# A static order of instructions, planned with a margin for other engines' answers and a longer load of the inverses' matrices

## The chip, the cores and the metric

The kernel runs on one core of a Trainium2 chip. Times are microseconds (us) on the device for one launch. Where one number stands for a kernel, it is the median of several runs. Engines: PE (TensorE, matmuls), DVE (VectorE), ACT (ScalarE), POOL (GpSimd) and SP (SyncE, which here issues the transfers). Each engine works off its own list of instructions in order.

## What is computed

One layer over 2048 tokens of width 1024, all in float32:

```
h = rms_norm(x);  proj = h @ w_in            # 17 chunks of 128 columns
A: sliding-window attention, 6 query heads, window 128, in blocks of 128 queries
B: RWKV-7 time mixing, 6 heads of 64: S = S*d + (S a) b^T + v k^T;  y = S r,  then GroupNorm, bonus, gate
M: cross-attention of 4 heads into 256 memory tokens
x = x + concat(A, B, M) @ w_out
u = rms_norm(x) @ w_up;  uc = conv3(u);  x = x + (silu(gate) * val) @ w_down     # 2816 columns wide
```

## The kernel before

Large products run in a split form: each float32 operand is cut into a high part (whi, hh, h2h, made by ACT) and a low part (wlo, hl, h2l, made by DVE as the rest), and three matmuls stand for one. The feed-forward products go by Strassen's scheme: seven products of half blocks (tiles uf, uch, uip in PSUM) for eight; DVE forms sums of weight pieces (ws) for them, and three buffers hold split weights.

The work has these stages. Up to about 1130 us the projections (tile mm), the attention (pl, lg, tpa, po) and the recurrence run together; the recurrence is cut into 16 blocks of 128 tokens, numbered 0 to 15 here. Then the output projection ends, its result is normalised, the feed-forward's up products run for the two halves of the tokens (44 units, each of which makes two chunks of columns) and last its down products.

In each block of the recurrence twelve small triangular matrices are inverted (rwkv_front_g). PE makes their products (pg), DVE masks them (gmk), two transfers lay them out in DRAM (nbd), and one transfer of 384 KB loads them as nb, with 96 partitions. The tile nb has one buffer, so a load can begin only when the inversion of the block before has read its last row. DVE then makes 31 steps, each one multiplication (xtmp, which reads nb) and one addition (xinv). The inverse goes out to DRAM (xbd), comes back (xa), and is used by the chain of the recurrence (pq, pu, pS, y).

The order of the instructions is static. The code does not call the engines; it records every operation with its engine, an estimated duration, and the operations that it depends on (class Recorder; cost gives the durations, and for a transfer the time that it needs on the way, lat). Then order gives each operation a level, the length of the longest path from it to the end, and run plans the engines in time: on each engine that is free it takes, of the operations that are ready by the plan, the one of the highest level. The program is emitted in that order; on the chip the real waits are made by semaphores. So the planner's numbers decide nothing but which instruction stands ahead of which. All instructions are issued from one line, the helper's call in emit (L345 in the profile), so tiles tell them apart, not lines.

Of a transfer the plan takes 900 + SLACK = 2400 ns after it has landed until what waits for it can start, and between engines the fixed answers of the table LAT, 110 to 287 ns.

Of the kernel before, what the change touches and what calls it, by code (L numbers as in the profile page):

```python
# [129 lines left out]
class Recorder:  # L130
# [40 lines left out]
    def add(self, eng, fn, a, k):  # L171
        outs = [v for v in (k.get("out"), k.get("accum_out")) if v is not None] or [a[0]]
        ins = [v for v in list(a) + list(k.values()) if isinstance(v, View) and not any(v is w for w in outs)]
        outs = [v for v in outs if isinstance(v, View)]
        dur, lat = cost(eng, fn, a, k)
        o = self._op(eng, fn, a, k, dur, lat)
        for v, w in [(v, False) for v in ins] + [(v, True) for v in outs]:
            t = v.t
            o.deps.add(t.pool.op)
            if not t.users:  # L180
                t.pool.rings.setdefault(t.tag or t.name, []).append(t)
            box = v.box if t.pool.space != PSUM else tuple((0, n) for n in t.shape)
            keep = []
            for p, b, pw in t.log:
                if (w or pw) and p is not o and all(x0 < y1 and y0 < x1 for (x0, x1), (y0, y1) in zip(b, box)):
                    o.deps.add(p)
                    if w and all(y0 <= x0 and x1 <= y1 for (x0, x1), (y0, y1) in zip(b, box)):
                        continue
                keep.append((p, b, pw))
            keep.append((o, box, w))  # L190
            t.log = keep
            if not t.users or t.users[-1] is not o:
                t.users.append(o)
                t.pool.users.append(o)
        return o
# [12 lines left out]
    def slots(self):  # L208

        for p in self.pools:  # L210
            for tag, ring in p.rings.items():
                held = []
                for t in ring:
# [7 lines left out]
                                u.deps.update(q.users)  # L221
                    held.append(t)

    def delay(self, o, s):
        if o.order or s.order:
            return 0
        return o.lat + 2000 + SLACK if o.lat else self.LAT[o.eng][s.eng]

    def order(self):

# [26 lines left out]
    def run(self):  # L257
        ops = self.ops
        left = {o: len(o.deps) for o in ops}
        now = {e: [] for e in self.ENG}  # L260
        soon = {e: [] for e in self.ENG}
        free = {e: 0.0 for e in self.ENG}
        hw = dma = 0.0
        out = []

        def release(o):

            o.ready = 0.0
            for d in o.deps:
                if d.order:  # L270
                    t = d.start
                elif o.order:
                    t = d.start
                else:
                    t = d.end + (900 + SLACK if d.lat else self.LAT[d.eng][o.eng])
                o.ready = max(o.ready, t)
            if o.eng is None:
                o.start = o.end = o.ready
                out.append(o)
                follow(o)  # L280
            else:
                heapq.heappush(soon[o.eng], (o.ready, o.n, o))

        def follow(o):
            for s in o.succ:
                left[s] -= 1
                if left[s] == 0:
                    release(s)

        for o in ops:  # L290
            if not o.deps:
                release(o)
        while True:
            best = None
            for e in self.ENG:
                if now[e]:
                    t = free[e]
                elif soon[e]:
                    t = max(free[e], soon[e][0][0])
                else:  # L300
                    continue
                if best is None or t < best[0]:
                    best = (t, e)
            if best is None:
                break
            t, e = best
            while soon[e] and soon[e][0][0] <= t:
                o = heapq.heappop(soon[e])[2]
                heapq.heappush(now[e], (-o.level, o.n, o))
            o = heapq.heappop(now[e])[2]  # L310
            if soon[e] and o.dur > 150:
                c = min((c for c in soon[e] if c[0] < t + min(WAIT, o.dur) and c[2].level > o.level), default=None)
                if c:
                    heapq.heappush(now[e], (-o.level, o.n, o))
                    free[e] = c[0]
                    continue
            o.start = t
            if o.lat:
                free[e] = t + (max(o.dur, DMAQ * o.lat) if e == "sync" else o.dur)
                hw = max(hw, t) + 475  # L320
                dma = max(dma, hw + 650) + o.lat
                o.end = dma + (500 if e == "gpsimd" else 0)
            else:
                o.end = free[e] = t + o.dur
            out.append(o)
            follow(o)
        assert len(out) == len(ops)
        return out
# [26 lines left out]


WAIT = 100
SLACK = 1500
WR = 4
WS = 3  # L360
# [13 lines left out]
def cost(eng, fn, a, k):  # L374

    out = k["out"] if "out" in k else a[0]
    n = math.prod(out.shape[1:])
    vecs = sum(isinstance(k.get(v), View) for v in ("scalar", "scalar1", "scalar2", "bias", "scale", "accum_out"))
    src = [v for v in (k.get("in_"), k.get("in0"), k.get("in1")) if isinstance(v, View)]
    psum = any(v.t.pool.space == PSUM for v in src + [out] if isinstance(v, View))  # L380
    if fn == "dma_start":
        v = out if isinstance(out, View) else k["in_"]
        size = max(4 * math.prod(v.shape), 20000)
        return (1050, size / 360) if eng == "gpsimd" else (60, size / 360)
    if eng == "tensor":
        if fn == "transpose":
            return 109, 0
        m, c = math.prod(a[1].shape[1:]), math.prod(a[2].shape[1:])
        if out.box[0][0] >= 64:
            return COL64, 0  # L390
        if a[1].dt == F32R:
            return max(c / 2.4, m / 1.2) + 14, 0
        return 2 * (max(c / 1.2, m / 1.2) + 2), 0
    if fn in ("reduce_max", "reduce_sum"):
        n = math.prod(k["in_"].shape[1:])
    if eng == "gpsimd":
        if k.get("op") == ALU.pow:
            return 300 + 165 * n, 0
        return (150 + 2.1 * n if fn == "tensor_tensor" else 122 + 0.6 * n), 0
    if eng == "scalar":  # L400
        return (50 if psum else 93) + 93 * vecs + n / 1.2, 0
    if fn in ("tensor_scalar", "tensor_copy") and not psum:
        n /= 2
    return 62 + 67 * vecs + n / 0.96 + (7 if fn == "tensor_tensor" else 0), 0
# [1296 lines left out]
```

## Time and profile before

| | us |
|---|---|
| runs | 2533.53, 2536.06 (median), 2548.08 |
| the profiled execution, its own time | 2532.01 |
| its span, first to last instruction | 2530.1 |
| PE busy | 2403.9 (95%) |
| DVE busy | 2037.7 (81%) |
| ACT busy | 1256.3 (50%) |
| mean granted clock of PE | 0.966 |

Busy time of an engine is the time in which it executes an instruction; matmuls overlap, so PE's busy time includes their pipelined ends. The granted clock is given as a share of 2.4 GHz; in any one moment it is either 1.00 or 0.50 (1.2 GHz), so a mean between them tells how long the engine ran at half speed. Stretches of the trace are counted in us from the start of the span.

### The profile page before, as it was taken

The page shows a single profiled execution, that of the slowest core. Times are in us where ns is not written, and L with a number is a line of the kernel's source. Part 1 is how long each engine was busy: PE and PEld are TensorE (multiplying, and loading weights), DVE is VectorE, ACT ScalarE, POOL GpSimd, SP SyncE. Part 2 cuts the span into 40 slices and gives each one's busy share as a digit, 9 for nine tenths or more (in the row PEclk, how much of TensorE's full clock was granted, in tenths as well). Part 3 has the DMA queues.
Part 4 walks back from the last instruction along what each step waited for, and adds up shares of the span by engine and source line. Part 5 has one row for each costly group of instructions (what it writes and reads, how often), then busy time and mean ns, then how long its engine had stood idle before and what let it go on. Part 6 is the DMA issues. An engine that isn't in the chain of part 4 may idle for free.

```text
span 2530.1 us, 36859 instructions
## 1 busy us (share of the span) xinstructions
PE 2403.9 (95%) x12268; PEld 1897.1 (75%) x12268; DVE 2037.7 (81%) x4901; ACT 1256.3 (50%) x2541; POOL 78.5 (3%) x53
## 2 busy tenths in 40 slices
PE   8898999899898989999899999999999998999999
PEld 6777777666676757667788788888888886887887
DVE  6677778778778777769688998899888888878876
ACT  5354544555445554555354455565545463444442
POOL 1111011010000010000000000000000000000000
PEclk9999999989989989999999999999999998999999
DMA  7675745744344464547323733353233256548543
GB/s 230 192 214 153 212 131 149 203 138 121 114 134 124 128 183 137 177 134 259 109 97 111 265 130 106 111 179 137 99 108 106 88 166 205 166 150 274 157 146 111
DMA packets 292935, 389.32 MB, mean 154 GB/s; under 512 B 49911, under 2 KB 155392, under 8 KB 292744
## 3 DMA queue, kind: packets, MB, share of 16 engines
q1 hardware_dynamic: 292744, 386.96, 49.1%
q8 instruction: 97, 1.59, 0.3%
q14 instruction: 94, 0.77, 0.1%
HBM read 274.89 MB, written 111.97 MB: 153 GB/s over the span
## 4 chain that ended last, share of the span: by engine, by line
PE 77%; DVE 9%; DMA 6%; issue 4%; ACT 3%; SPq 0%; POOL 0%; POOLq 0%; DVEq 0%; ACTq 0%
PE uf L345 27%; PE mm L345 15%; PE uch L345 13%; PE uip L345 6%; PE pq L345 4%; DMA nb<-nbd 3%; PE pg L345 2%; PE po L345 2%; DMA wraw<-w_ip_in 2%; DVE wlo L345 1%; DVE uc L345 1%; PE pl L345 1%; PE tpa L345 1%; DVE h2l L345 1%; PE pu L345 1%
## 5 line engine op out<-in xcount | busy, mean ns | idle before, releaser
L345 ACT CAST whi<-wraw 128x512 fp32r<-128x512 f32 (+1 forms) x410 | 250.3, 613 | 367.8 <-PE mm L345 135.2
L345 PE MATMUL uf<-h2h,wlo 128*128 128x512 f32 x1056 | 412.4, 392 | 14.1 <-DVE wlo L345 14.1
L345 PE MATMUL uf<-h2h,whi 128*128 128x512 f32 x1056 | 413.9, 392 | 8.5 <-ACT whi L345 6.0
L345 PE MATMUL uf<-h2l,whi 128*128 128x512 f32 x1056 | 413.0, 391 | 0.0
L345 DVE TENSOR_TENSOR wlo<-wraw,whi 128x512 fp32r<-128x512 f32 (+1 forms) x410 | 277.3, 679 | 101.5 <-ACT whi L345 99.6
L345 ACT CAST whi<-ws 128x512 fp32r<-128x512 f32 (+1 forms) x272 | 164.8, 609 | 348.8 <-PE uf L345 163.7
L345 DVE SCALAR_TENSOR_TENSOR uc<-ub,pp,uc 128x1024 f32<-128x1024 f32 x176 | 225.0, 1282 | 26.2 <-ACT uc L345 25.2
L345 PE MATMUL mm<-hh,whi 128*128 128x512 f32 x544 | 226.7, 418 | 18.6 <-ACT whi L345 6.6
L345 PEld LDWEIGHTS uf<-h2h,wlo 128*128 128x128 f32 x1056 | 199.6, 189 | 57.0 <-DVE wlo L345 15.1
L345 PEld LDWEIGHTS uf<-h2h,whi 128*128 128x128 f32 x1056 | 199.4, 189 | 53.9 <-ACT whi L345 8.1
L345 PEld LDWEIGHTS uf<-h2l,whi 128*128 128x128 f32 x1056 | 199.6, 189 | 41.7 <-DVE h2l L345 0.7
L345 PE MATMUL mm<-hh,wlo 128*128 128x512 f32 x544 | 221.9, 409 | 1.4 <-DVE wlo L345 1.4
L345 PE MATMUL mm<-hl,whi 128*128 128x512 f32 x544 | 223.0, 410 | 0.0
L345 PE MATMUL uch<-h2h,whi 128*128 128x512 f32 x528 | 205.7, 390 | 0.1
L345 PE MATMUL uch<-h2h,wlo 128*128 128x512 f32 x528 | 205.8, 390 | 0.0
L345 PE MATMUL uch<-h2l,whi 128*128 128x512 f32 x528 | 205.5, 389 | 0.0
L345 DVE TENSOR_TENSOR wlo<-ws,whi 128x512 fp32r<-128x512 f32 (+1 forms) x272 | 181.3, 672 | 23.3 <-ACT whi L345 22.0
L345 PEld LDWEIGHTS mm<-hh,whi 128*128 128x128 f32 x544 | 105.9, 195 | 47.1 <-ACT whi L345 8.8
L345 ACT CAST h2h<-tr 128x512 fp32r<-128x512 f32 x182 | 110.3, 620 | 58.5 <-DMA tr<-dg 35.4
L345 DVE TENSOR_TENSOR xtmp<-xinv,nb 96x60 f32<-96x60 f32 (+24 forms) x496 | 100.7, 203 | 38.7 <-DMA nb<-nbd 34.5
L345 DVE TENSOR_TENSOR h2l<-tr,h2h 128x512 fp32r<-128x512 f32 x182 | 120.3, 688 | 9.2 <-ACT h2h L345 9.1
L345 ACT ACTIVATE uc<-ub,pp 128x1024 f32<-128x1024 f32 x88 | 109.7, 1247 | 34.0 <-DVE ub L345 32.9
(366 smaller groups left out, 4721.5 us busy)
## 6 DMA issues: line engine op xcount, KB each, us to landing
wraw<-w_up_in SPq DMA_DIRECT2D x176, 256.0 KB
tr<-dg SPq DMA_DIRECT2D x154, 256.0 KB
wraw<-w_ip_in SPq DMA_DIRECT2D x136, 256.0 KB
dg<-uc SPq DMA_DIRECT2D x88, 256.0 KB
dg<-tt SPq DMA_DIRECT2D x66, 256.0 KB
wraw<-w_op_in SPq DMA_DIRECT2D x64, 256.0 KB
wraw<-w_down_in SPq DMA_DIRECT2D x64, 256.0 KB
xk<-xT_in SPq DMA_DIRECT2D x56, 256.0 KB
```

What stands on the lines that cost most here:

```text
L345: getattr(getattr(nc, o.eng), o.fn)(*map(real, o.a), **{k: real(v) for k, v in o.k.items()})
```

## The change

Two numbers of the planner's model change, and the way in which a long transfer takes up the queue. Between operations of different engines a margin of 300 ns is added to the answer, both in the levels and in the plan. The load of nb gets 2500 ns more on its way; of any transfer's time only 2200 ns occupy the transfers that come after it.

```diff
+    def margin(self, d, o):
+
+        return 0 if d.eng == o.eng or None in (d.eng, o.eng) else MARGIN
+
     def delay(self, o, s):
         if o.order or s.order:
             return 0
-        return o.lat + 2000 + SLACK if o.lat else self.LAT[o.eng][s.eng]
+        return o.lat + 2000 + SLACK if o.lat else self.LAT[o.eng][s.eng] + self.margin(o, s)
...
-                    t = d.end + (900 + SLACK if d.lat else self.LAT[d.eng][o.eng])
+                    t = d.end + (900 + SLACK if d.lat else self.LAT[d.eng][o.eng] + self.margin(d, o))
...
-                dma = max(dma, hw + 650) + o.lat
-                o.end = dma + (500 if e == "gpsimd" else 0)
+                dma = max(dma, hw + 650) + min(o.lat, 2200)
+                o.end = dma + max(0, o.lat - 2200) + (500 if e == "gpsimd" else 0)
...
+MARGIN = 300
...
+        if v.t.name == "nb":
+            return 60, size / 360 + 2500
```

The same instructions are issued, in another order on every engine. Two places show it. The first is DVE in the recurrence, where the inversion of block 5 begins. In the rows, xtmp and xinv are the inversion's steps, nb with its number is the loaded matrix; y, rq_t, rq_y, S0, gam and el belong to the norm and the state of the recurrence, rsb to the attention, wlo, qlo and lo3 are low parts. Between the last xtmp of block 4 and the first of block 5 stand 18 instructions before. These are the last twelve rows of that stretch before:

```order
L345 TENSOR_TENSOR rq_t_4818<-rq_t_4818,rq_y_4809 128x6
L345 TENSOR_TENSOR S0_112<-S0_112,gam_3693 64x3x64
L345 TENSOR_TENSOR vt_4943<-tpv_4871,vm_4905 128x512
L345 TENSOR_SCALAR ss_4926<-ss_4926 128x1
L345 SCALAR_TENSOR_TENSOR rq_y_4809<-rq_t_4818,rq_y_4809 128x6
L345 TENSOR_TENSOR S0_112<-S0_112,gam_3693 64x3x64
L345 TENSOR_TENSOR rq_t_4818<-rq_h_4806,rq_y_4809 128x6
L345 TENSOR_TENSOR rq_t_4818<-rq_t_4818,rq_y_4809 128x6
L345 SCALAR_TENSOR_TENSOR rq_y_4809<-rq_t_4818,rq_y_4809 128x6
L345 TENSOR_TENSOR wlo_4967<-wraw_4837,whi_4955 128x512
L345 TENSOR_TENSOR qlo_4972<-mm_4890,qhi_4965 128x512
L345 TENSOR_TENSOR xtmp_4980<-xinv_4197,nb_4913 96x31
```

With the change 35 instructions stand between the two, and these are the last twelve rows:

```order
L349 TENSOR_TENSOR gam_4558<-el_4583,em__5052 128x3
L349 COPY el_5329<-ep_5042 128x3
L349 TENSOR_TENSOR rq_t_5294<-rq_t_5294,rq_y_5289 128x6
L349 TENSOR_SCALAR rsb_1625<-sx_5265 128x4x2
L349 SCALAR_TENSOR_TENSOR rq_y_5289<-rq_t_5294,rq_y_5289 128x6
L349 TENSOR_SCALAR rsb_1625<-sx_5246 128x4x2
L349 TENSOR_TENSOR qlo_5339<-kp_5291,qhi_5319 128x512
L349 SCALAR_TENSOR_TENSOR y_4943<-y_4943,rq_y_5289,lnw_387 128x64
L349 CAST lo3_5331<-qlo_5339 32x512
L349 SCALAR_TENSOR_TENSOR y_4943<-y_4943,rq_y_5289,lnw_387 128x64 x5
L349 TENSOR_TENSOR y_4943<-y_4943,bv_4812 128x384
L349 TENSOR_TENSOR xtmp_5380<-xinv_4380,nb_5296 96x31
```

The first step of the new inversion has moved back: the end of the norm (the six rows on y and the addition of bv) stands ahead of it now.

The second place is DVE in the feed-forward's first half, where the second half's tokens are normalised (rows uc<-uc,pp, tt) beside the running up products. wlo and ws are pieces of weights that PE waits for, uc<-ub the convolution. Before:

```order
L345 SCALAR_TENSOR_TENSOR uc_15187<-ub_14960,pp_118,uc_15187 128x1024
L345 SCALAR_TENSOR_TENSOR uc_15209<-ub_15094,pp_118,uc_15209 128x1024
L345 TENSOR_TENSOR ws_15241<-ws_15193,wraw_14995 128x512
L345 SCALAR_TENSOR_TENSOR uc_15209<-ub_15094,pp_118,uc_15209 128x1024
L345 SCALAR_TENSOR_TENSOR uc_15196<-uc_15196,pp_118,uc_15064 128x1024
L345 TENSOR_TENSOR uc_15187<-uc_15187,uc_15209 128x1024
L345 TENSOR_TENSOR tt_15261<-uc_15196 128x512
L345 TENSOR_TENSOR tt_15265<-uc_15187,tt_15214 128x512
L345 TENSOR_TENSOR uc_15046<-uc_15187,uc_15046 128x512
L345 TENSOR_TENSOR tt_15273<-uc_15187,tt_15265 128x512
L345 TENSOR_TENSOR wlo_15277<-ws_15241,whi_15247 128x512
```

With the change:

```order
L349 SCALAR_TENSOR_TENSOR uc_15194<-ub_14960,pp_118,uc_15194 128x1024
L349 SCALAR_TENSOR_TENSOR uc_15228<-ub_15101,pp_118,uc_15228 128x1024
L349 SCALAR_TENSOR_TENSOR uc_15177<-uc_15177,pp_118,uc_15071 128x1024
L349 SCALAR_TENSOR_TENSOR uc_15228<-ub_15101,pp_118,uc_15228 128x1024
L349 TENSOR_TENSOR tt_15269<-uc_15177 128x512
L349 TENSOR_TENSOR uc_15194<-uc_15194,uc_15228 128x1024
L349 TENSOR_TENSOR wlo_15276<-ws_15203,whi_15224 128x512
L349 TENSOR_TENSOR tt_15280<-uc_15194,tt_15180 128x512
L349 TENSOR_TENSOR uc_15040<-uc_15194,uc_15040 128x512
L349 TENSOR_TENSOR tt_15286<-uc_15194,tt_15280 128x512
L349 TENSOR_TENSOR wlo_15292<-ws_15188,whi_15242 128x512
```

A wlo has moved into the middle of the pile. Before, fifteen instructions stand between this wlo and the one ahead of it; with the change the longest such stretch around the normalising has ten.

## Rows read from the trace of the kernel before

**Rows 1.** Busy time of each engine (us, instructions), PE's clock, transfers, two stages.
```profile
core 0: us, PE busy (x) PEld busy (x) DVE busy (x) ACT busy (x) POOL busy (x), PEclk, DMA share, GB/s
...
160.00:1050.00 890.00, 820.96 (x5114) 608.18 (x5113) 698.26 (x2652) 457.09 (x1213) 55.09 (x25) 0.93 0.53 151
1050.00:1240.00 190.00, 174.01 (x923) 133.11 (x921) 134.39 (x300) 95.81 (x214) 3.78 (x3) 0.93 0.54 176
```

**Rows 2.** Waits of DVE: us in total, times, longest us.
```profile
DVE xtmp L345 <- DMA nb<-nbd: 34.5, 14, 4.1
```

**Rows 3.** Chain that ended last, at block 5: start us, us, what.
```profile
438.44 7.41 DMA nb<-nbd
...
446.78 0.59 ACT sh L345
```

**Rows 4.** DVE in order of time: blocks 3, 5 (two rows), 15; idle before, releaser.
```profile
344.73 0.19 DVE L345 TENSOR_TENSOR xtmp<-xinv,nb 96x31 f32<-96x31 f32 x1 [4.13 <-DMA nb<-nbd]
...
437.56 0.16 DVE L345 TENSOR_TENSOR xtmp<-xinv,nb 96x8 f32<-96x8 f32 x1
...
445.87 0.19 DVE L345 TENSOR_TENSOR xtmp<-xinv,nb 96x31 f32<-96x31 f32 x1 [2.48 <-DMA nb<-nbd]
...
1025.35 0.18 DVE L345 TENSOR_TENSOR xtmp<-xinv,nb 96x31 f32<-96x31 f32 x1 [3.89 <-DMA nb<-nbd]
```

**Rows 5.** PE in order of time, behind the load of block 5.
```profile
447.42 0.80 PE L345 MATMUL mm<-hh,whi 128*128 128x512 f32 x1 [5.81 <-ACT sh L345]
```

**Rows 6.** Busy time and clock, 30 us behind each load, blocks 0 to 15.
```profile
171.00:201.00 30.00, 27.12 (x121) 21.43 (x120) 24.45 (x90) 14.38 (x26) 8.40 (x2) 1.00 0.53 152
227.00:257.00 30.00, 24.83 (x136) 20.04 (x135) 22.54 (x82) 12.53 (x29) 3.27 (x3) 0.83 0.52 147
293.00:323.00 30.00, 28.93 (x217) 21.35 (x216) 23.11 (x74) 16.75 (x42) 0.00 (x0) 0.94 0.59 170
342.00:372.00 30.00, 27.46 (x174) 20.63 (x172) 25.23 (x90) 17.23 (x42) 8.79 (x2) 0.94 0.46 140
398.00:428.00 30.00, 27.50 (x198) 21.98 (x197) 23.83 (x87) 14.37 (x35) 5.38 (x4) 0.94 0.48 150
443.00:473.00 30.00, 25.58 (x123) 20.86 (x124) 21.87 (x74) 14.13 (x30) 0.64 (x1) 0.89 0.69 187
511.00:541.00 30.00, 27.13 (x188) 20.55 (x189) 20.50 (x93) 18.55 (x59) 6.83 (x1) 0.83 0.43 127
561.00:591.00 30.00, 24.85 (x132) 15.79 (x132) 24.76 (x127) 17.39 (x56) 0.00 (x0) 0.89 0.30 89
629.00:659.00 30.00, 29.64 (x229) 21.71 (x228) 24.65 (x102) 16.62 (x51) 0.18 (x1) 1.00 0.39 116
675.00:705.00 30.00, 23.56 (x100) 13.71 (x98) 22.19 (x112) 14.46 (x49) 0.92 (x1) 0.68 0.33 96
750.00:780.00 30.00, 30.00 (x219) 21.65 (x218) 23.44 (x95) 15.38 (x43) 0.00 (x0) 1.00 0.34 105
799.00:829.00 30.00, 24.70 (x129) 15.55 (x128) 23.76 (x115) 14.61 (x48) 0.00 (x0) 0.83 0.38 105
868.00:898.00 30.00, 30.00 (x212) 21.63 (x211) 23.61 (x98) 17.18 (x49) 0.00 (x0) 1.00 0.37 98
916.00:946.00 30.00, 23.94 (x96) 16.57 (x97) 23.92 (x90) 18.77 (x52) 0.00 (x0) 0.74 0.87 250
981.00:1011.00 30.00, 30.00 (x209) 22.50 (x208) 24.11 (x90) 13.18 (x32) 0.00 (x0) 1.00 0.40 131
1020.00:1050.00 30.00, 26.78 (x150) 20.75 (x148) 25.43 (x115) 16.68 (x51) 0.00 (x0) 0.94 0.63 177
```

**Rows 7.** Busy time and clock, three stretches of the feed-forward.
```profile
1396.00:1412.00 16.00, 11.61 (x40) 8.74 (x39) 16.00 (x24) 4.67 (x8) 0.00 (x0) 0.79 0.71 228
1412.00:2084.00 672.00, 671.63 (x2961) 555.03 (x2960) 600.67 (x931) 362.50 (x535) 0.00 (x0) 1.00 0.39 133
2084.00:2106.00 22.00, 10.29 (x34) 7.96 (x33) 21.27 (x33) 9.65 (x15) 0.00 (x0) 0.69 0.59 192
```

## The prediction

> **What bounds the kernel now.** I read the stages first. From 160 to 1050 us, where the projections, the attention and the recurrent blocks run together, TensorE (PE) is busy 820.96 of 890 us, at a mean granted clock of 0.93 [rows 1]. Busy time times clock is work at full speed: 820.96 x 0.93 = 763.5, so 126.5 us are lost there to waits and to the half clock. In the feed-forward stretch from 1412 to 2084 us PE is busy 671.63 of 672 us at clock 1.00 [rows 7]: an order can win nothing there, only lose. So the change has to earn its time before 1240 us, or at the few marred places after it.
>
> Next, who makes the first of these stages wait. VectorE (DVE) waits 34.5 us in 14 places for one kind of transfer, the load of nb [rows 2]. DVE is in-order and busy 698.26 of 890 us [rows 1], so such a wait holds up all that stands behind. Block 5 shows it. Its load starts at 438.44 and lands 7.41 us later [rows 3]. The inversion before it makes its last step at 437.56; DVE then has work up to 443.4, and stands still for 2.48 us until the first step with the new matrix, at 445.87 [rows 4]. The chain of waits goes from there by way of a sum on DVE, which stood behind that step, to a copy on ScalarE (ACT) at 446.78 [rows 3], for whose answer PE has been idle 5.81 us when it goes on at 447.42 [rows 5].
>
> Then what such a wait costs PE. I cut 30 us behind each of the sixteen loads, from about 5 us after its issue [rows 6], and take 30 minus busy time times clock. In order of the blocks the loss is 2.9, 9.4, 2.8, 4.2, 4.2, 7.2, 7.5, 7.9, 0.4, 14.0, 0, 9.5, 0, 12.3, 0 and 4.8 us, together 87 of the 126.5. The four windows behind the blocks 8, 10, 12 and 14, which wait little or not at all, lose 0.4 us in all: PE can run there at full clock with the same mix of work. The other twelve lose 7.2 each. A wait of two to four us thus brings a loss that is larger than the wait, because the clock drops too: in block 9's window it is 0.68.
>
> **The change, part by part.** No instruction is added or removed; only the order on each engine changes, so the terms are waits.
>
> *The load of nb.* There is one buffer for nb, so a load can start only when the previous inversion has read its last row. For the blocks 3, 5, 7, 9, 11, 13 and 15 this is what binds: the cover is the DVE work between the last xtmp of one inversion and the first of the next. Counted in the built orders that is 12, 18, 21, 14, 27, 15 and 20 instructions before, and 21, 35, 32, 28, 34, 23 and 28 with the change: 127 and 201. In block 5 the instructions from 437.56 to 443.4 took 5.8 us [rows 4], or about 0.32 us each, so the seven covers grow by 74 x 0.32 = 23.7 us, 2.2 to 5.4 us each. The seven waits are 20.6 us together (the first and the last, 4.13 and 3.89 us, in [rows 4]). Block by block the growth covers all of it in 5, 7, 9 and 13, and leaves about 1.2, 0.9 and 1.3 us in 3, 11 and 15: 3.4 us remain, 17.2 go.
>
> The other nine blocks wait 13.9 us. In eight of them the binding piece is the way from the last gmk to the first xtmp; it holds 301 instructions before and 316 with the change, about 0.6 us more each. In block 1 the load now stands behind the previous inversion, with ten instructions between. I let 9 of these 13.9 us stand.
>
> In PE time: the five windows of blocks 5, 7, 9, 11 and 13 lose 7.2 + 7.9 + 14.0 + 9.5 + 12.3 = 50.9 us, two thirds of those of 3 and 15 are 6, and 3 us come from the even blocks: 60 us if all loss in those windows hangs on the load. The other bound is that only the wait itself is won and neither the clock nor what follows: 17 us. Some waits in these windows are of the attention's own chain, so neither end is likely; I take the middle, -38 us.
>
> What holds the new place up: if the covering work were itself late, the wait would only move to it. It is work of the norm (y and its reciprocal root), which needs no transfer, so I let it stand at nothing.
>
> On a rule of the Trainium skill, which speaks against this part: "DMA: Bandwidth & Descriptors", section "Anatomy of one DMA", puts a transfer at about 2.0 us plus its bytes at 436 GB/s; for this load of 384 KB that is an estimate of 2.9 us. By it the old cover of 5.8 us was enough, the longer transfer in the planner would be a false figure, and the term would be nothing. The page's fit is for transfers issued by GpSimd; here the issue is SyncE's, and the trace has 7.41 us, so the measurement decides.
>
> *The margin of 300 ns.* It moves every answer between engines. PE's waits under the load's shadow are the 87 us above; outside those windows the two stages up to 1240 us lose 126.5 - 87 = 39.5 and 190 - 174.01 x 0.93 = 28 us [rows 1]. I see no single place in the order that wins or loses these 68 us. I take nothing, with a quarter of them, 17 us, to either side.
>
> *Feed-forward, normalising the second half.* At 1396 to 1412 us DVE is busy all 16.00 us with 24 instructions, 0.67 us each, while PE loses 16 - 11.61 x 0.79 = 6.8 us [rows 7]. A product is twelve matmuls; at 671.63 / 2961 = 0.227 us each (the steady stretch) it takes 2.72 us, and three buffers of split weights make a reserve of 8.2 us. Before, fifteen DVE instructions stand between two wlo, 10 us: more than the reserve. With the change the most is ten, 6.7 us: less. I take -6, with 0 and -6.8 as bounds.
>
> *From up to down.* At 2084 to 2106 us PE loses 22 - 10.29 x 0.69 = 14.9 us [rows 7]. The pile of DVE work ahead of the first wlo of the down products stays, and grows from 24 to 26 instructions, at 21.27 / 33 = 0.64 us each: +1.5.
>
> Sum: -38 - 6 + 1.5 = -42.5. The profiled execution took 2532.0 us (span 2530.1), 4 us under the median of the three runs. 2532 - 42.5 + 4 gives 2494.
>
> **The rivals.** (1) The load is covered, but the loss in those windows belongs to the attention's chain of answers. Then only the waits are won: -17 - 3 + 1.5, so 2517. For it: a wait of two to four us is a small part of the 7.2 us that such a window loses. Against it: the four good windows hold the same chain and lose 0.4 us.
> (2) No change: what the load no longer holds up waits for something else on DVE's queue, or the loads land later still because others were moved ahead of them on SyncE's queue; also the skill's figure, which would make the first term nothing (I give that 0.04 within this case). 2532. For it: DVE is busy 78% of the stage, so little room is left for what moves. Against: the sixteen windows show DVE as busy in the good ones (23 to 25 us of 30) as in the bad.
> (3) Slower, in the steady feed-forward. From 1412 to 2084 us one pair of columns takes seven products, 19.04 us; 35 of them fit. If the margin had moved wlo in every unit so that PE waits 1.6 us in each, 35 x 1.6 = 56 us would be added, at DVE's 89% with no room to catch up: 2494 + 56 = 2550. It decides once more DVE work than the reserve of 8.2 us stands between two wlo of a unit. Against it: counted in the order, the most in a steady unit is seven to ten instructions, 5 to 7 us. The unit's 100% is what a reshuffle can only harm, and that speaks for it.
>
> **How the numbers follow.** My forecast, 2494, has 0.50; rival (1) 0.17; (2) 0.18; (3) 0.15. A measurement here can tell about 0.5%, 12.7 us, from no change. Forecast and (1) are faster: 0.67; (2) is the same: 0.18; (3) slower: 0.15. The lower end takes all upper bounds: 60 + 6.8 + 17 = 84 less 1.5, so 2453; I take 2454. The upper end has to take in (2) and the nearer part of (3): 2546. That leaves about 0.07 below and 0.12 above. The forecast's own range is 2454 to 2516.
>
> **What would show it.** Right: DVE's waits for nb near 12 us instead of 34.5, mostly in blocks 0 to 3; the mean clock from 160 to 1050 us at 0.95 or more, and PE losing under 3 us in windows cut behind the loads of blocks 5, 7, 9 and 13; no wait of PE near the second half's normalising; the wait at the first down product still 11 to 14 us. Wrong: the waits for nb gone and the clock still 0.93 (then rival 1, or the waits moved to lg and tpa); or PE under 99% in the steady feed-forward (rival 3); or the load landing over 9 us after its issue.

## The result, and the profile after

The changed kernel takes 2503.39 us (median of four runs, 2500.96 to 2505.86); the kernel before, run beside it, 2540.39. The ratio is 0.9865, 95% interval 0.9839 to 0.9890: 1.35% faster, about 34 us. The forecast was 2494 in 2454 to 2546. The profiled execution took 2500.96 us, its span 2499.2; against the profile of before that is 31 us less, where the sum was -42.5. So the time is close. What follows shows that the two terms behind it were not.

First the page of the changed kernel, its row of busy times:

```profile
PE 2371.0 (95%) x12268; PEld 1880.6 (75%) x12268; DVE 2043.6 (82%) x4901; ACT 1251.7 (50%) x2541; POOL 83.0 (3%) x53
```

PE is busy 32.9 us less than before, with the same instructions. Where, a table by stage says. I cut it at the first matmul of the feed-forward (tile uf), which starts at 1239.0 us before and at 1213.1 now. The kernel before, its stages ahead of that matmul, and its last down products:

```profile
0.00:1239.00 1239.00, 1135.88 (x6724) 853.81 (x6724) 937.61 (x3166) 630.50 (x1575) 78.45 (x53) 0.94 0.55 164
...
2106.00:2530.10 424.10, 417.54 (x1831) 341.79 (x1829) 334.45 (x558) 169.03 (x294) 0.00 (x0) 1.00 0.55 173
```

The changed kernel, the same two and the stretches that answer to [rows 1] and [rows 7]:

```profile
0.00:1213.10 1213.10, 1105.04 (x6724) 836.60 (x6724) 943.11 (x3166) 628.70 (x1575) 83.00 (x53) 0.95 0.56 167
160.00:1050.00 890.00, 818.64 (x5318) 610.74 (x5317) 727.07 (x2714) 471.50 (x1251) 57.85 (x25) 0.95 0.54 157
...
1370.10:1386.10 16.00, 13.86 (x53) 10.60 (x53) 15.92 (x24) 5.82 (x9) 0.00 (x0) 0.89 0.68 229
1386.10:2058.10 672.00, 672.00 (x2963) 555.66 (x2962) 602.27 (x929) 361.25 (x534) 0.00 (x0) 1.00 0.40 133
2058.10:2080.10 22.00, 9.10 (x30) 6.97 (x29) 21.86 (x34) 9.67 (x14) 0.00 (x0) 0.69 0.58 192
...
2080.10:2499.20 419.10, 414.50 (x1826) 341.95 (x1824) 332.48 (x555) 167.40 (x294) 0.00 (x0) 1.00 0.54 175
```

Ahead of the feed-forward 25.9 us are won. PE's idle time there is the stretch less its busy time: 103.1 us before, 108.1 now. It did not shrink; the busy time of the same 6724 matmuls did, by 30.8 us. Part of that is the clock: by the granted clock in the trace, 118.6 us of the busy time ran at the lower level before and 97.5 with the change, and half of the difference, 10.5 us, is time given back. Counted at full speed (the part at the lower level halved) the busy time falls from 1076.6 to 1056.3 us, by 20.3. At the second half's normalising PE loses 16 - 13.86 x 0.89 = 3.7 us (before 6.8), in the transition to the down products 22 - 9.10 x 0.69 = 15.7 (before 14.9), in the last stage 4.6 us of waits are left of 6.6. The steady stretch stays full.

VectorE's waits for the load of nb, the answer to [rows 2]:

```profile
DVE xtmp L349 <- DMA nb<-nbd: 13.8, 7, 4.5
```

34.5 us became 13.8, in blocks 0, 2, 3, 4, 5, 13 and 15; the forecast was near 12. Yet the windows behind the loads, cut as in [rows 6], hardly improve. These are those of blocks 3, 5, 7, 9, 10, 13 and 14:

```profile
360.70:390.70 30.00, 23.09 (x116) 18.23 (x115) 25.01 (x94) 13.95 (x36) 5.45 (x4) 0.83 0.49 155
...
475.00:505.00 30.00, 21.84 (x119) 15.98 (x117) 25.07 (x117) 16.75 (x54) 9.27 (x2) 0.83 0.77 183
...
575.80:605.80 30.00, 26.37 (x157) 18.11 (x156) 26.95 (x113) 17.75 (x55) 1.64 (x1) 0.89 0.50 143
...
679.00:709.00 30.00, 22.77 (x117) 16.32 (x116) 28.84 (x119) 13.38 (x45) 0.00 (x0) 0.73 0.53 145
740.80:770.80 30.00, 28.89 (x227) 20.64 (x226) 24.81 (x99) 17.21 (x49) 0.00 (x0) 1.00 0.42 133
...
890.60:920.60 30.00, 22.95 (x84) 15.23 (x84) 24.21 (x95) 16.39 (x48) 0.00 (x0) 0.73 0.84 231
958.10:988.10 30.00, 30.00 (x214) 23.70 (x213) 24.21 (x90) 16.21 (x36) 0.00 (x0) 1.00 0.44 133
```

30 less busy time times clock gives for the sixteen blocks 1.4, 1.3, 0, 10.8, 0, 11.9, 3.3, 6.5, 3.0, 13.4, 1.1, 3.3, 1.8, 13.2, 0 and 3.0 us, together 74 where it was 87. The windows of 5, 7, 9 and 13, forecast under 3 us each, lose 11.9, 6.5, 13.4 and 13.2. Block 9 no longer waits for nb at all. What PE waits for there, in order of time (start, length, what, and in brackets the idle time before it and who ended it):

```profile
683.72 0.50 PE L349 MATMUL mm<-hh,whi 128*128 128x512 f32 x1 [2.85 <-DVE sh L349]
...
693.12 0.80 PE L349 MATMUL pl<-ka,dq 128*128 128x256 f32 x2 [1.04 <-DVE lg L349]
694.89 0.80 PE L349 MATMUL pl<-ka,dq 128*128 128x256 f32 x2 [0.98 <-DVE lg L349]
698.32 0.85 PE L349 MATMUL p<-xT,ND 64*64 64x32 f32 x12 [1.37 <-DVE xT L349]
```

All four wait for VectorE, which is busy 28.84 of these 30 us (before, in [rows 6], 22.19); of the two waits left out, 0.53 us is for a transfer (ka) and 0.34 us for VectorE. Here PE waits for VectorE itself, without the load. It is not so in every window: in block 5's, the longest wait is 3.57 us for ScalarE (whi), and the next 2.30 us for the transfer of ka. The clock follows; the same stretch by two windows:

```profile
683.70:692.70 9.00, 7.44 (x32) 5.55 (x32) 8.10 (x35) 2.60 (x5) 0.00 (x0) 1.00 0.77 208
692.70:709.80 17.10, 14.26 (x68) 9.94 (x69) 16.59 (x74) 9.87 (x38) 0.00 (x0) 0.50 0.30 82
```

PE was busy 7.44 of 9 us, then ran 17.1 us at the lower level. A last thing from the chain of waits, which goes through four of the loads: two of them took much longer than the 7.41 us of [rows 3], those of block 5 and block 15.

```profile
470.05 9.61 DMA nb<-nbd
...
995.21 10.50 DMA nb<-nbd
```

### The profile page after: what moved, and what is told of

It reads as the page before. It is cut to its first block, busy times and chain, and to the rows that moved or that the text cites. A ratio compares the mean times of both kernels' runs of the same rounds, so it can differ in the third digit from the quotient of the medians.

```text
span 2499.2 us, 36814 instructions
## 1 busy us (share of the span) xinstructions
PE 2371.0 (95%) x12268; PEld 1880.6 (75%) x12268; DVE 2043.6 (82%) x4901; ACT 1251.7 (50%) x2541; POOL 83.0 (3%) x53
## 4 chain that ended last, share of the span: by engine, by line
PE 76%; DVE 12%; DMA 5%; issue 3%; ACT 2%; SPq 0%; POOL 0%; POOLq 0%; DVEq 0%; ACTq 0%
PE uf L349 28%; PE uch L349 14%; PE mm L349 13%; PE uip L349 7%; PE pq L349 4%; PE pg L349 2%; DMA nb<-nbd 1%; PE po L349 1%; DVE wlo L349 1%; DVE xinv L349 1%; DVE xtmp L349 1%; DMA wraw<-w_ip_in 1%; PE pl L349 1%; DVE lg L349 1%; PE tpa L349 1%
## 5 line engine op out<-in xcount | busy, mean ns | idle before, releaser
L349 ACT ACTIVATE uc<-ub,pp 128x1024 f32<-128x1024 f32 x88 | 109.5, 1244 | 35.9 <-DVE ub L349 35.1
L349 PEld LDWEIGHTS mm<-hl,whi 128*128 128x128 f32 x544 | 105.4, 194 | 25.8 <-issue 3.7
```

The source lines that it names most:

```text
L349: getattr(getattr(nc, o.eng), o.fn)(*map(real, o.a), **{k: real(v) for k, v in o.k.items()})
```

## The experiments

Theory A is the prediction's: the cover of the load makes the gain. Theory B, formed on the rows above: the margin makes it, in PE's busy time. Theory C: any new order falls somewhere, and neither part does what it says. The table gives each run's ratio to the kernel before that ran beside it, PE's idle and busy time ahead of the feed-forward (from the same kind of row as above), the busy time at full speed as counted above, VectorE's waits for nb, and how often two successive matmuls of that stretch differ in the shape of the stationary block (128\*128, 64\*64, 128\*64 and so on, counted in the trace), which the last experiments brought up. The time is a median of four to ten runs, the columns from idle on are from one profiled execution each. Intervals stand in the text.

| kernel | us | ratio | idle | busy | at full speed | nb waits | shape changes |
|---|---|---|---|---|---|---|---|
| before (profile) | 2532 | 1 | 103.1 | 1135.9 | 1076.6 | 34.5 | 883 |
| the change | 2503.4 | 0.9865 | 108.1 | 1105.0 | 1056.3 | 13.8 | 752 |
| load alone | 2508.2 | 0.9886 | 92.0 | 1123.6 | 1066.1 | 5.7 | 814 |
| margin alone | 2516.6 | 0.9922 | 114.2 | 1110.5 | 1049.0 | 43.7 | 718 |
| before, no wait for nb | 2523.9 | 0.9944 | 95.7 | 1132.1 | 1076.6 | 0 | 883 |
| change, no wait for nb | 2499.5 | 0.9847 | 98.2 | 1109.1 | 1056.0 | 0 | 752 |
| control 1 (slack) | 2540.8 | 1.0004 | 106.8 | 1145.7 | 1061.5 | 33.4 | 817 |
| control 2 (wait) | 2556.2 | 1.0100 | 111.5 | 1152.5 | 1070.7 | 29.5 | 870 |
| change, margin 150 | 2481.5 | 0.9777 | 90.9 | 1101.5 | 1054.6 | 7.9 | 769 |
| change, margin 600 | 2513.2 | 0.9906 | 106.6 | 1107.8 | 1039.2 | 9.3 | 698 |
| change, load +4000 | 2493.2 | 0.9829 | 101.3 | 1103.8 | 1053.7 | 4.4 | 750 |
| margin in the plan only | 2497.0 | 0.9863 | 85.5 | 1119.1 | 1058.6 | 6.3 | 814 |
| before, PE stays at a tile | 2482.5 | 0.9805 | 109.5 | 1081.5 | 1033.3 | 32.9 | 620 |
| load alone, PE stays | 2462.1 | 0.9708 | 90.4 | 1081.1 | 1033.4 | 6.9 | 629 |

The busy time at full speed goes with the order: the two pairs of kernels with one order (with and without the wait for nb) agree in it within 0.3 us.

**The two parts apart.** The load alone. The limit of 2200 ns goes with it, since the planner's time for the next longest transfer (768 KB) is 2185 ns:

```diff
...
-MARGIN = 300
+MARGIN = 0
...
```

> The change without its margin (MARGIN 0): only the longer load of nb is planned. Theory A, that of the prediction: the cover of the load makes the gain, so this alone brings most of the 31 to 37 us, 2505 to 2515 us, and VectorE's waits for nb fall from 34.5 us to under 18. Theory B, formed on the trace of the changed kernel: the sixteen windows behind the loads give back only 13 of 87 us, the rest comes from the margin, so this alone brings 5 to 15 us, 2522 to 2535. Theory C: any other set of numbers shuffles the order anew, and the time falls where it falls, not tied to the waits for nb.

Measured: 2508.22 us, ratio 0.9886 (0.9856 to 0.9916). By stage, and VectorE's waits:

```profile
0.00:1215.61 1215.61, 1123.64 (x6724) 846.37 (x6725) 942.88 (x3167) 630.54 (x1575) 79.64 (x53) 0.95 0.57 167
```

```profile
DVE xtmp L349 <- DMA nb<-nbd: 5.7, 7, 1.9
```

The margin alone:

```diff
...
-        if v.t.name == "nb":
-            return 60, size / 360 + 2500
...
```

> The margin of 300 ns, without the longer load of nb. Theory A: 2525 to 2540 us, at most the 4 to 6 us of the feed-forward's normalising, with VectorE's waits for nb still over 25 us. Theory B: 15 to 30 us faster than before, 2508 to 2523, with PE's busy time in the stages before the feed-forward some 20 us (at full clock) below that of before, whatever the waits for nb do. Theory C: not foreseen by either.

Measured: 2516.59 us, ratio 0.9922 (0.9888 to 0.9957).

```profile
0.00:1224.66 1224.66, 1110.50 (x6724) 845.71 (x6725) 939.01 (x3166) 630.04 (x1575) 81.94 (x53) 0.94 0.56 166
```

```profile
DVE xtmp L349 <- DMA nb<-nbd: 43.7, 16, 4.7
```

Each alone wins, and by another way. The load takes 11 us of idle time and 12 of busy time (10.5 at full speed). The margin makes the waits for nb longer, 43.7 us against 34.5, and idle time 11 us longer, and wins all the same, since busy time falls by 25 us (27.6 at full speed). Theory A is right on the first kernel and wrong on the second, theory B the reverse; together they do not add up (29 and 20 us apart, 34 together).

**The price of the wait itself.** The inversion's multiplications read a constant in nb's place; the inverses are then other numbers. The order is that of before, instruction by instruction.

```diff
...
-        real = lambda v: v.real() if isinstance(v, View) else v
+        real = lambda v: getattr(v, "alt", v).real() if isinstance(v, View) else v
...
-            dv.tensor_tensor(out=tmp[:, :nj, :w], in0=x[:, :nj, s:s + 1].broadcast_to([96, nj, w]),
-                            in1=nb[:, s:s + 1, s + 1:].broadcast_to([96, nj, w]), op=ALU.mult)
+            v = nb[:, s:s + 1, s + 1:].broadcast_to([96, nj, w])
+            v.alt = self.c["x0"][0:96].rearrange("p (j t) -> p j t", j=8)[:, 0:1, 0:w].broadcast_to([96, nj, w])
+            dv.tensor_tensor(out=tmp[:, :nj, :w], in0=x[:, :nj, s:s + 1].broadcast_to([96, nj, w]), in1=v, op=ALU.mult)
...
```

> The order of the kernel before, but the multiplications of the inversion read a constant in place of nb (the inverses come out as other numbers; nb is still loaded), so that VectorE never waits for nb. Theory A: the waits of 34.5 us and what hangs on them go, 35 to 55 us faster, 2483 to 2505, and the windows behind the loads of blocks 5, 7, 9 and 13 lose under 4 us each. Theory B: those windows lose for other answers too, so 5 to 17 us faster, 2520 to 2535.

Measured: 2523.85 us, ratio 0.9944 (0.9924 to 0.9964), 14 us.

```profile
0.00:1227.80 1227.80, 1132.08 (x6724) 852.68 (x6725) 938.34 (x3167) 629.49 (x1575) 78.56 (x53) 0.95 0.56 165
```

This is the cleanest number of the study, since no order changed: 34.5 us of VectorE's waiting are worth 14 us. Ahead of the feed-forward 11.2 us go, 7.4 of them idle time of PE (103.1 to 95.7) and 3.8 the clock (110.9 us of busy time at the lower level, before 118.6). Theory B had it. The windows decide it as well, cut like those of [rows 6], from about 5 us after each issue of the load. These are those of blocks 5, 7, 9 and 13, which theory A put under 4 us each:

```profile
433.40:463.40 30.00, 25.88 (x107) 21.12 (x108) 21.32 (x74) 14.05 (x30) 0.64 (x1) 0.89 0.69 183
...
553.30:583.30 30.00, 25.66 (x128) 16.30 (x127) 24.14 (x122) 16.72 (x55) 0.00 (x0) 0.78 0.29 86
...
668.00:698.00 30.00, 24.50 (x136) 15.84 (x134) 27.54 (x131) 16.14 (x54) 1.64 (x1) 0.89 0.40 118
...
900.50:930.50 30.00, 20.24 (x81) 14.19 (x81) 24.02 (x85) 17.30 (x47) 1.71 (x1) 0.76 0.90 250
```

They lose 7.0, 10.0, 8.2 and 14.6 us, and the sixteen together still 73 of the 87. So most of the loss in them never hung on the load. (The loads themselves can start earlier here, since no instruction reads nb; that is the one other thing that differs.) The same in the order of the change:

> The order of the changed kernel, with the same replacement: the 13.8 us of waits for nb that it still has go too (the inverses come out as other numbers). Theory A: 13 to 20 us faster than the changed kernel, 2483 to 2490. Theory B: at most 6 us faster, 2497 to 2503; the windows behind the loads of blocks 9 and 13, which lose 13 us each with 0 and 1.2 us of wait, stay as they are.

Measured: 2499.47 us, ratio 0.9847 (0.9817 to 0.9877), about 4 us under the change. The 13.8 us still waited are worth that and no more: theory B again, though the two intervals overlap. The windows of blocks 9 and 13 still lose 14 and 13 us, as theory B said.

**Controls and doses.** Is an order worth something by chance? The kernel before, with SLACK at 1600 in place of 1500, and with WAIT at 120 in place of 100:

> A control: the kernel before, with one number of the planner changed that has nothing to do with the two of the change (the slack after every transfer, 1500 to 1600 ns), so that the order is shuffled anew without a reason. If the two parts of the change work by what they do (theory B: the load's cover closes waits, the margin packs small matmuls), this stays within 8 us of before, 2531 to 2548, and PE's busy time at full clock before the feed-forward within 6 us of before. By theory C (the time falls where a new order happens to fall) it can be 10 to 30 us away from before, to either side.

Measured: 2540.82 us, ratio 1.0004 (0.9979 to 1.0029); its ten runs lie between 2517 and 2547.

```profile
0.00:1252.51 1252.51, 1145.67 (x6724) 864.83 (x6725) 939.49 (x3167) 630.09 (x1575) 82.09 (x53) 0.92 0.54 162
```

The time is as theory B has it. Its other condition, busy time at full clock within 6 us of before, fails: at full speed it is 15 us below, with 66 changes of shape fewer. That did not show in the time, since 168.4 us of busy time ran at the lower level in place of 118.6; as it stands the busy time is 10 us above before.

> A second control: the kernel before, with the planner's wait for a more urgent operation at 120 in place of 100 ns, so that the order is shuffled anew without a reason (1397 changes of tile, before 1391). If a new order alone is worth nothing: 2528 to 2548, as the first control (2541). If orders are a lottery with a width of tens of us: over 15 us away from before.

Measured: 2556.22 us, ratio 1.0100 (1.0075 to 1.0124): 22 us slower.

```profile
0.00:1263.98 1263.98, 1152.51 (x6724) 866.73 (x6725) 939.81 (x3167) 632.16 (x1575) 79.28 (x53) 0.92 0.55 160
```

The edit has no purpose, but the trace says where the time went: idle time is 8 us longer, and 163.5 us of busy time ran at the lower level in place of 118.6, which costs another 22; at full speed busy time is 6 us shorter. So a new order alone can be worth 1%, here mostly by the clock, and theory C is not empty: a single comparison of two orders that differ by less says little on why. What holds is what repeats, or what is far above 1%.

The margin at 150 and at 600, with the load as in the change:

> The changed kernel with half the margin, 150 ns. Theory B: between the load alone (2508) and the change (2503), 2502 to 2512, with PE's busy time at full clock before the feed-forward between those of the two kernels (about 1060 of 1066 and 1055 us). Theory C: anywhere from 2490 to 2530, in no order with the margin.

Measured: 2481.54 us, ratio 0.9777 (0.9750 to 0.9805).

> The changed kernel with twice the margin, 600 ns. Theory B: PE's busy time at full clock before the feed-forward falls below 1055 us or stays, and the time is 2490 to 2505; a loss of over 10 us would need waits elsewhere (a margin that keeps ready work back). Theory C: anywhere from 2490 to 2530.

Measured: 2513.23 us, ratio 0.9906 (0.9882 to 0.9930). Margins of 0, 150, 300 and 600 thus give 0.9886, 0.9777, 0.9865 and 0.9906: no order in the time, as theory C says. Margin 600 has the fewest changes of shape of the four and 17 us less busy time at full speed than the change, but 137.2 us of it at the lower level in place of 97.5 (clock 0.93, the other three 0.95), so it reaches the feed-forward at 1214.4 us, as late as the change at 1213.1. What makes it slower is the feed-forward itself, 1298.8 us in place of 1286.1, with 9.4 us more idle time of PE. Margin 150 differs from 300 in idle time ahead of the feed-forward, 90.9 us in place of 108.1. That it is better by a cause, and not by the width that the controls show, is not settled.

The load with 4000 in place of 2500 ns:

> The changed kernel with 4000 ns in place of 2500 added to the load of nb. Theory A and B alike: VectorE's waits for nb fall from 13.8 us to under 8, which by the run without any wait for nb (4 us below the changed kernel) is worth at most 4 us: 2497 to 2505. Theory C: the waits fall and the time goes anywhere from 2490 to 2530.

Measured: 2493.17 us, ratio 0.9829 (0.9802 to 0.9857); one wait of 4.4 us is left. Four us better than foreseen by A and B, within what chance gives.

**What is in the busy time.** PE's busy time takes in the pipelined ends of matmuls, so it can hold waits that no idle time shows. In the kernel before, PE in order of time, where products of the recurrence (pq) stand between transposes (tpy) and the attention (pl), and six us on where pq stands alone:

```profile
751.86 0.44 PE L345 MATMUL tpy<-cst,y 128*128 128x128 f32 x2
752.23 0.33 PE L345 MATMUL pq<-uv,gmk 64*64 64x64 f32 x2
752.48 0.33 PE L345 MATMUL tpy<-cst,y 128*128 128x128 f32 x1
752.74 0.33 PE L345 MATMUL pq<-uv,gmk 64*64 64x64 f32 x2
753.00 0.38 PE L345 MATMUL pl<-ka,dq 128*128 128x256 f32 x1
...
758.07 1.05 PE L345 MATMUL pq<-uv,gmk 64*64 64x64 f32 x12
759.05 0.66 PE L345 MATMUL tpv<-cst,sh 128*128 128x128 f32 x4
759.47 0.47 PE L345 MATMUL mm<-hh,whi 128*128 128x512 f32 x1
```

Twelve pq in one run take 0.98 us from their start to the next, 0.082 each; four tpv 0.42, 0.105 each. Mixed, two pq and one tpy take 0.51 us (752.23 to 752.74), where 2 x 0.082 + 0.105 = 0.27 would do. Nothing is idle there by the profile, yet half of it is lost, at two changes. So I gave the planner of the kernel before one more rule:

```diff
...
             o = heapq.heappop(now[e])[2]
+            if e == "tensor":
+                same = [c for c in now[e] if tile_of(c[2]) is last and c[2].level > o.level - STICK]
+                if tile_of(o) is not last and same:
+                    heapq.heappush(now[e], (-o.level, o.n, o))
+                    c = min(same)
+                    now[e].remove(c)
+                    heapq.heapify(now[e])
+                    o = c[2]
...
             o.start = t
+            if e == "tensor":
+                last = tile_of(o)
...
+STICK = 3000
+
+
+def tile_of(o):
+    return (o.k["out"] if "out" in o.k else o.a[0]).t
...
```

> The kernel before, without margin and without the longer load, with one new rule in the plan: TensorE, where it may choose, stays at the tile of its last matmul unless other ready work is over 3000 ns more urgent. By count of the built orders TensorE then goes from one tile to another 1063 times before the feed-forward, before 1391, with the change 1305. Theory D (the margin's gain is that TensorE changes tiles less often, and the fill and short waits at a change stand in its busy time): busy time before the feed-forward falls by 25 us or more from 1135.88, and the kernel comes to 2490 to 2520. Rival E (the changes of tile cost nothing; what the margin brings is another thing): busy time within 8 us of before, 2528 to 2550, or slower, since urgent work waits.

Measured: 2482.49 us, ratio 0.9805 (0.9786 to 0.9825), twice the width of the controls. By stage, and the waits:

```profile
0.00:1190.99 1190.99, 1081.51 (x6724) 834.08 (x6725) 934.78 (x3167) 627.74 (x1575) 78.73 (x53) 0.95 0.58 170
```

```profile
DVE xtmp L356 <- DMA nb<-nbd: 32.9, 14, 3.3
```

Busy time falls by 54 us (43.3 at full speed, the rest is the clock), the waits for nb stay as they were, idle time is 6 us longer: theory D, some 8 us under the range that it gave, and a larger gain than the whole change, with neither of its two numbers. The trace then corrected the theory in one point. Over three kernels (before, the change, this one), at full clock and where no idle time is shown, I compared the interval from one matmul's start to the next with that inside a run of the same kind. At 1939 places where the shape of the stationary block changes it is 91 ns longer on the average; at 1198 places where only the tile changes it is not longer at all (27 ns shorter). So the price is on the change of shape. The interval behind that one is longer too: against runs of one shape from their fourth matmul on, the interval at a change of shape is 103 ns longer (1819 places) and the next 51 ns (1772 places), about 0.15 us together; at a change of tile alone the two cancel (21 ns shorter, 24 longer). Two other ways give the same. 263 fewer changes at 0.15 us make 40 of the rule's 43.3 us. And over the twelve orders in the table, controls included, busy time at full speed falls by 0.16 us for each change fewer (correlation 0.98). The rule itself holds PE to a tile; one that holds it to a shape wasn't run. The Trainium skill, "TensorEngine Tiling (Array Packing)", section "Tiling Modes", says that switching the tiling mode, not just the tile, drains TensorE. The intervals agree in that the shape costs and the tile does not; whether each change of shape here is a change of that mode, the profile does not tell.

The margin in the plan alone:

```diff
...
-        return o.lat + 2000 + SLACK if o.lat else self.LAT[o.eng][s.eng] + self.margin(o, s)
+        return o.lat + 2000 + SLACK if o.lat else self.LAT[o.eng][s.eng]
...
```

> The changed kernel with the margin in the planned time alone, none in the levels. Theory F (what counts is that the plan holds back work whose operand has only just been made): the gain stays, 2495 to 2512. Rival G (what counts is that the levels rank long chains through many engines higher): it falls back to the load alone, 2506 to 2520, with busy time before the feed-forward near the 1124 us of that run.

Measured: 2497.00 us, ratio 0.9863 (0.9841 to 0.9886). The time is that of theory F, the busy time that of G: changes of shape stay at 814, as with the load alone, and busy time at 1119, while idle time falls to 85.5. So the margin in the levels is what lowers the changes of shape (to 752) and brings idle time back, to 108.1; in time that comes to nothing here. At full speed busy time is 7.5 us below that of the load alone, with as many changes of shape: the count does not explain everything, and what did this is open. The levels' half alone wasn't run.

Last, the load and the new rule, without a margin:

> The longer load of nb without a margin, together with the rule that TensorE stays at its tile (1089 changes of tile before the feed-forward). If the load's gain is idle time (11 us less idle in the run with the load alone) and the rule's gain is busy time (54 us less in the run with the rule alone), the two add up: idle time before the feed-forward about 92 us in place of 109.5, and 2465 to 2478, with the margin not needed. If they share one cause, or the rule holds back what the inversion waits for, no better than the rule alone: 2478 to 2495.

Measured: 2462.10 us, ratio 0.9708 (0.9681 to 0.9734), the fastest of all, about 40 us under the change.

```profile
0.00:1171.48 1171.48, 1081.06 (x6724) 830.62 (x6725) 936.08 (x3167) 629.09 (x1575) 78.14 (x53) 0.95 0.59 173
```

The two gains add up nearly, 74 us where 29 and 50 were won alone, 3 us more than the forecast range had. Not by their parts, though: on top of the rule the load takes 19 us of idle time (109.5 to 90.4) and nothing of busy time, where alone it took 11 and 12.

## Why the prediction was right in its time, and wrong in its terms

**The load of nb, -38.** The waits came out as said in their sum (13.8 us, near 12), but not by blocks: 7.3 us in the odd blocks from 3 on, where 3.4 were forecast, and 6.5 in the others, where 9 were. The price of them did not come out. The step that failed is the one from the windows: because the four good windows lose nothing, the whole loss of the others was hung on the load, and the middle of 17 and 60 taken. Without any wait for nb the old order wins 14 us, under the lower bound of 17, and its sixteen windows still lose 73 of 87 us. Those of the change lose 74. In these last PE waits 46.9 us in all, 32.8 of them for VectorE (lg, the inversion's xinv, sh, xk and others), 11.3 for ScalarE and 2.8 for a transfer. Rival (1), that the loss belongs to other answers, was nearer here, and so was a part of rival (2): in block 9 PE waits for VectorE's own queue. The load's edit as a whole wins in each of the three pairs (29 us alone, 14 on top of the margin, 25 on top of the new rule). Of the 23.4 us that it wins alone ahead of the feed-forward, 11.1 are idle time and 10.5 busy time at full speed, for which 69 fewer changes of shape at 0.15 us are enough; the rest is the clock. That an order with fewer such changes came out of it is chance, as far as the record goes: on top of the margin the edit made 34 more, and on top of the new rule 9 more.

**The margin, 0 ± 17.** The term was put at nothing. Alone the margin wins 20 us, and on top of the load 5, both within the 22 us of the second control; the busy time at full speed, 27.6 us lower alone, is not (the controls: 15 and 6). The step that failed stands in the first paragraph of the prediction: busy time times clock was taken for work at full speed, a fixed amount, so that only idle time and half clock could be won. Ahead of the feed-forward the same matmuls are busy 1076.6 us at full speed before and 1056.3 with the change. 131 fewer changes of shape at 0.15 us make these 20 us. The clock gives 10.5 more, and idle time takes 4.9 back: 25.9 together. Why a margin leads the planner to fewer changes of shape is not shown; the run with the margin in the plan only says that it comes by the levels.

**The feed-forward.** The normalising was given -6 and brought -3.1: a wait of 2.1 us for wlo remains, though by count the longest pile of DVE work ahead of one is shorter than the reserve. The transition was given +1.5 and brought +0.8. The last stage, not spoken of, gave 2 us. Rival (3) did not come: the steady stretch is busy 672.00 of 672.

**The sum.** As a forecast for the stage ahead of the feed-forward, -38 was about 12 too large: 25.9 us were won there, 13 of them in the windows, and as much outside, where the forecast had nothing. The time was right by luck: a term that was too large stood in for one that was missing.

**The signs named.** Waits for nb near 12 us, mostly in blocks 0 to 3: 13.8, of which 7.4 there. Clock 0.95 from 160 to 1050 us: yes. Under 3 us in the windows of 5, 7, 9 and 13: no. No wait near the normalising: no. The wait at the first down product at 11 to 14 us: yes, 12.9. Loads under 9 us: two were longer.

## What to carry to other kernels

Before a stage is called bound by waits, look at the busy time of the engine itself: count it at full speed, from the granted clock. If the same instructions can be busy for fewer microseconds in another order, busy time is not work, and an order in which TensorE changes the shape of its stationary block less often is worth trying before any finer margin. Price a wait by taking it away in an unchanged order; here 34.5 us of waiting were worth 14. And where a planner's numbers reshuffle everything, run a number that means nothing too: here one such number moved the time by 1%, and a difference that is smaller explains nothing by itself.

## What was not expected of the hardware

A change of the stationary block's shape between two matmuls made the interval at it 91 to 103 ns longer on the average at full clock, by the reference that one takes, and the next one 51 ns, with no idle time shown; a change of the output tile within one shape cost nothing. After 9 us in which PE was busy 7.44, it ran 17.1 us at 1.2 GHz. In the second control 45 us more of the busy time than before ran at that level, which cost it 22 us. The load of 384 KB took 7.41 us from issue to landing in [rows 3], 9.61 and 10.50 in the rows of the change.
